# Joining the two halves of an attention value product: two scalar-engine copies and two vector additions from PSUM, or four copies and one addition in SBUF

## The chip, the cores and the metric

The kernel runs on one core of a Trainium2 chip. The core has five engines that run side by side, each with its own in-order queue: the tensor engine TensorE (PE in the profile, with PEld for its weight loads), the vector engine VectorE (DVE), the scalar engine ScalarE (ACT), GpSimdE (POOL) and the sync engine SyncE (SP), which only issues DMAs here. TensorE writes its products to PSUM, a small memory of banks of 128 x 512 float32; DVE and ACT read PSUM, POOL does not. Everything else works on SBUF. The metric is the device time of one execution in microseconds (us), less is better; the time of a kernel is the median of its runs.

## The reference

One decoder layer over 1024 tokens with 1024 channels. Its two token mixers run in parallel from one input projection: sliding-window attention (16 query heads, 4 key/value heads of width 64, window 128, one sink logit per head) and a gated delta rule (8 heads of width 128). Both are projected, gated, summed and projected again, and a squared-ReLU MLP follows. What matters here is the attention:

```python
def _sliding_window_attention(q, k, v, sinks):
    ...
    kb, vb = band(k), band(v)                 # each block of 128 tokens sees itself and the block before
    scores = jnp.einsum('bnqhgd,bnshd->bnhgqs', qb, kb).astype(jnp.float32) * (ATT_HEAD_DIM ** -0.5)
    ...
    m = jnp.maximum(jnp.max(scores, axis=-1, keepdims=True), sink)
    p = jnp.exp(scores - m)
    denom = jnp.sum(p, axis=-1, keepdims=True) + jnp.exp(sink - m)
    probs = (p / denom).astype(v.dtype)
    o = jnp.einsum('bnhgqs,bnshd->bnqhgd', probs, vb)
    return o.reshape(b, s, ATT_Q_W)
```

The last product, `probs` times `vb`, is the one whose result is joined.

## The kernel before

The kernel reaches float32 accuracy with a faster matmul format by splitting: a tensor is kept as a high part and a low part (the remainder), and a product is three matmuls (high by high, high by low, low by high). ACT copies the high part, DVE subtracts to get the low one.

**The stage.** The attention is not a stage of its own. It is woven into a long run of projections (`stream_unit`, 26 units of 48 matmuls of 128 x 512 on the three PSUM banks called `mm`; line 248). `count[0]` is the number of such matmuls issued so far, and it is the clock of the program: `at(p, f)` puts a function into a heap under the count `p`, `after(n, f)` puts it `n` counts on, and `run_events` calls what is due before each projection matmul. So the order on TensorE, DVE and ACT is written out by hand through these numbers (`manual_schedule`); POOL's order is left to the framework's scheduler.

**A slot.** There are 64 slots, one for each pair of heads `j = s // 8` and block of 128 queries `n = s % 8`, 16 counts apart. A slot has three parts on TensorE, each with its followers on the other engines:

- `att_scores(s)` at the slot's count: four matmuls into a bank of tag `a` (two banks; lines 834 and 835), then `top` (DVE, masks and takes the maximum, `nscore`, line 842), `expo` (ACT, exponentials, line 849), `join` (POOL, adds the two halves of the window, `sm`, line 853), `inv` (DVE, reciprocal of the sum, line 856) and `scale` (ACT, line 861).
- `att_turn(s)` at +28: two transposes of `sm` into a bank of tag `b` (two banks; line 877), then the high copy (ACT, `ph`, line 883), the low part (DVE, line 887) and a masked copy `pl` (POOL, line 894).
- `att_values(s)` at +62: the product with the values into the only bank of tag `c` (line 909): two matmuls with `ph` and, for `n > 0`, two with `pl`. It is this product that is joined.

**The value product and its join.** The left operand of line 909 is a tile of 128 columns: 64 columns are the high part of the values and 64 are the low part. So rows 0 to 63 of the bank hold one partial sum and rows 64 to 127 the other, for two heads side by side (columns 0 to 127 and 128 to 255), and the answer is their sum. The kernel does this with an ACT copy and two DVE additions:

```python
def top():
    A.activation(out=bot, in_=av[64:128, 0:256], func=AF.Copy)          # line 914
    after(4, join)
def join():
    ...
    for i in range(2):
        V.tensor_tensor(out=o[64 * i:64 * i + 64, (n % 2) * P:(n % 2 + 1) * P],   # line 922
                        in0=av[0:64, i * P:(i + 1) * P], in1=bot[:, i * P:(i + 1) * P], op=ALU.add)
```

`o` is a 128 x 256 tile `at` that takes the two heads of two slots; on every odd slot POOL issues a DMA of it to DRAM (`attn_d`, line 925). `bot` and `at` have two buffers each.

**What else is in DVE's queue in this stage.** Low parts of weights (`wl`, line 216) and of queries (`qs`, line 803), and the steps of a triangular solve (`stt`, line 732, and `M`, line 737), 128 rows by up to about a thousand elements, which are strewn over the same counts.

After slot 63, `open_pc` releases these pools, DVE clears a tile there (`TT`, line 965), and the delta-rule heads begin.

Of the kernel before, what the change touches and what calls it, by code (L numbers as in the profile page):

```python
# [9 lines left out]
F32 = mybir.dt.float32  # L10
F32R = mybir.dt.float32r
BF16 = mybir.dt.bfloat16
AF = mybir.ActivationFunctionType
ALU = mybir.AluOpType
# [3 lines left out]
P = 128  # L18
# [16 lines left out]
def hybrid_layer_kernel(ctx: ExitStack, tc: tile.TileContext,  # L35
                        x, c, w_ada, b_ada, w_in, conv_w, a_log, dt_bias, sinks, dn_norm_w,
                        w_oa, w_ob, w_out, ln1_g, ln1_b, w_ff1, b_ff1, w_ff2, b_ff2,
                        ln2_g, ln2_b, out, dbg=None):
    nc = tc.nc
    x, c, out = x[0], c[0], out[0]  # L40
# [6 lines left out]
    V, A, G, T = nc.vector, nc.scalar, nc.gpsimd, nc.tensor  # L47
# [7 lines left out]
    def psum(tag, bufs, name=None):  # L55
        return ps.tile([P, HALF], F32, tag=tag, bufs=bufs, name=name or tag)
# [4 lines left out]
    def bc(ap, shape):  # L61
        return ap.to_broadcast(shape)
# [134 lines left out]
    def at(p, f, *args):  # L197
        order[0] += 1
        heapq.heappush(events, (p, order[0], f, args))

    def after(n, f, *args):
        at(count[0] + n, f, *args)
# [275 lines left out]
    for step in ('t0 s0 o00 o01 w0 w1 d4 t1 s1 v203 o10 v235 o11 v256 m0 t2 p2 s2 v304 o20 v346 o21 m1 t3 p3 s3 v404 o30 v446 o31 m2 '  # L478
                 't4 p4 s4 v504 o40 v546 o41 m3 t5 p5 s5 r0 v604 o50 v646 o51 m4 t6 p6 s6 v704 o60 v746 o61 m5 t7 p7 s7 o70 o71 m6').split():
        f, k = step[0], int(step[1])  # L480
# [44 lines left out]
    with tc.tile_pool(name="pa", bufs=2, side="right") as pa:  # L525
        if True:
# [76 lines left out]
            for half in range(2):  # L603
                gr = psum("a", 2)
                for j in range(4):
# [3 lines left out]
                                in1=gT[0:8, halves[half]].bitcast(F32), op=ALU.subtract)  # L609
# [42 lines left out]
        for h in range(8):  # L652
# [7 lines left out]
            for half in range(2):  # L660
                tp = psum("c", 1) if half else psum("b", 2)
                for j in range(4):
                    n = 4 * half + j
                    T.transpose(tp[:, j * P:(j + 1) * P], kT[:, n * P:(n + 1) * P], ident)
                for j in range(4):
                    n = 4 * half + j
# [11 lines left out]
            for half in range(2):  # L678
                V.tensor_tensor(out=kd[:, halves[half]].rearrange("p (n c) -> p n c", n=4),
                                in0=tps[half].rearrange("p (n c) -> p n c", n=4),  # L680
                                in1=bc(kdc[:, 4 * half:4 * half + 4, h:h + 1], [P, 4, P]), op=ALU.mult)
            (nc.sync if h == 7 else nc.gpsimd).dma_start(out=kd_d[h], in_=kd)
            for half in range(2):
                kk = psum("a", 2)
                for j in range(4):
                    n = 4 * half + j
                    kc = kT[:, n * P:(n + 1) * P]
                    T.matmul(kk[:, j * P:(j + 1) * P], lhsT=kc, rhs=kc, start=True, stop=True)
                for j in range(4):
                    n = 4 * half + j  # L690
# [20 lines left out]
    pb = pb_pool.__enter__()  # L711
# [104 lines left out]
    att = {}  # L816
# [84 lines left out]
    def att_values(s):  # L901
        j, n = s // 8, s % 8
        full, part = att.pop(s)
        av = psum("c", 1)
        vt = vhl[j // 2]
        prods = [(VB[n], full)] + ([(n, part)] if n else [])
        for b, p_ in prods:
            for m in range(2):
                T.matmul(av[:, 0:256], lhsT=vt[:, b, :], rhs=p_[:, m, :], start=p_ is full and m == 0,  # L909
                         stop=p_ is prods[-1][1] and m == 1)  # L910
        bot = pb.tile([64, 256], F32, tag="bot", name="bot")

        def top():
            A.activation(out=bot, in_=av[64:128, 0:256], func=AF.Copy)
            after(4, join)

        def join():
            if n % 2 == 0:
                att["at"] = pb.tile([P, 2 * P], F32, tag="at", name="at")
            o = att["at"]  # L920
            for i in range(2):
                V.tensor_tensor(out=o[64 * i:64 * i + 64, (n % 2) * P:(n % 2 + 1) * P],
                                in0=av[0:64, i * P:(i + 1) * P], in1=bot[:, i * P:(i + 1) * P], op=ALU.add)
            if n % 2 == 1:
                nc.gpsimd.dma_start(out=attn_d[j, :, (n - 1) * P:(n + 1) * P], in_=o)

        after(5, top)

    def slot(s):
        return int(SLOT0 + SLOT * s)  # L930
# [1 line left out]
    for s in range(64):  # L932
        at(slot(s), att_scores, s)
        at(slot(s) + TURN, att_turn, s)
        at(slot(s) + VAL, att_values, s)
# [568 lines left out]
    for s in range(4):  # L1504
# [4 lines left out]
        for ts in groups:  # L1509
            pts = []  # L1510
            for t in ts:
                tag = ("mm", "a", "mm", "c", "mm", "a")[bank % 6]
# [135 lines left out]
    def acc_tag(i, ab):  # L1648
        if i < EARLY:
            return {"A": "mm" if i < 3 else "b", "B": "aacaa"[i], "C": "caaca"[i]}[ab]  # L1650
        return {"A": "mm", "B": "a", "C": "b"}[ab]
# [203 lines left out]
    for i, m in seq:  # L1855
# [4 lines left out]
        if begin:  # L1860
            tag = acc_tag(i, ab)
# [146 lines left out]
```

## Time and profile before

| | |
|---|---|
| median of 3 runs | 1879.66 us (1875.06 to 1884.38) |
| the profiled execution | 1881.81 us, its span 1880.1 us |
| granted TensorE clock over the span | 0.99 |
| busy time of PE, DVE, ACT, POOL | 1826.4, 1306.0, 977.6, 339.2 us |
| first and last start of a `ph` matmul of the value product (line 909) | 257.4 and 568.9 us |
| matmuls of the value product (`ph`, `pl`) | 128 and 112 |
| ACT copies of line 914 | 64, 64 x 256, 382 ns each |
| DVE additions of line 922 | 128, 64 x 128, 278 ns each |
| DMA issues of `attn_d` (line 925) | 32 |

The span is from the first to the last instruction; what the execution's own time has beyond it lies around them. A group's row in the profile reads: line, engine, operation, output <- inputs, shapes, count | busy us, mean ns of one | idle time of that engine before them and what ended it. A row of the timeline reads: start us, us until the end, engine, line, operation, tiles, shapes, count, and in brackets the idle time before it with its releaser. Matmul ends are modelled: a 128 x 512 matmul shows 0.39 us, and yet the next one starts some 0.23 us after it. A row of the waits reads: who waited <- for whom: us in total, times, longest.

### The profile page before, as it was taken

Reading aid. Unit: us, or ns where it says so; the run is one execution under the profiler, and the core shown is the slowest. Engines: PE = TensorE matmul, PEld = TensorE weight load, DVE = VectorE, ACT = ScalarE, POOL = GpSimd, SP = SyncE. Lnnn points to the kernel's source line nnn. Section 1 sums busy time; section 2 is a strip of 40 time slices with the busy share of each in tenths; the row PEclk is TensorE's granted clock in tenths of the full one; section 3 lists DMA queues with packets and bytes.
Section 4 is the critical chain, followed back from the end, with each engine's and each line's share of the span. In section 5 each row is a group of like instructions: output and inputs, shape, how many; then the busy total and the mean of one; then the engine's idle time right before and its main releaser. Section 6 shows DMA issues by size and latency. Waiting matters only on the chain.

```text
span 1880.1 us, 26086 instructions
## 1 busy us (share of the span) xinstructions
PE 1826.4 (97%) x9161; PEld 1507.9 (80%) x9161; DVE 1306.0 (69%) x2473; ACT 977.6 (52%) x2105; POOL 339.2 (18%) x493
## 2 busy tenths in 40 slices
PE   7999999999999999999999999999999999999997
PEld 5877878878787878888878888877878787888886
DVE  7777588898875566666553445787867776576697
ACT  3689656666664454454553332465545555334441
POOL 7323323443331000000001110001221220000000
PEclk8999999999999999999999999999999999999999
DMA  9655642232248444544345644358978779755571
GB/s 260 171 183 199 214 100 77 84 98 70 68 170 227 127 139 134 159 149 144 118 157 187 205 141 151 123 168 279 311 240 282 261 244 396 281 196 170 198 259 45
DMA packets 262414, 337.74 MB, mean 180 GB/s; under 512 B 26005, under 2 KB 171110, under 8 KB 262026
## 3 DMA queue, kind: packets, MB, share of 16 engines
q1 hardware_dynamic: 222954, 212.94, 36.1%
q0 software_dynamic: 31328, 108.44, 17.1%
q10 hardware_dynamic: 8000, 14.68, 2.1%
q8 instruction: 72, 1.18, 0.3%
q14 instruction: 60, 0.49, 0.1%
HBM read 231.40 MB, written 102.51 MB: 178 GB/s over the span
## 4 chain that ended last, share of the span: by engine, by line
PE 77%; DVE 10%; DMA 5%; ACT 4%; issue 3%; SPq 1%; POOL 0%; ACTq 0%; DVEq 0%; POOLq 0%
PE mm L248 31%; PE mm L1929 6%; PE mm L1869 5%; PE b L1929 4%; PE a L1929 4%; PE b L1869 3%; PE c L1929 2%; PE a L1869 2%; PE mm L1499 2%; PE c L909 1%; DMA sraw<-in_w_ff_dram 1%; DVE wl L216 1%; PE mm L188 1%; PE mm L187 1%; PE mm L186 1%
## 5 line engine op out<-in xcount | busy, mean ns | idle before, releaser
L248 PE MATMUL mm<-uh,wl 128*128 128x512 f32 x800 | 332.3, 415 | 0.0
L248 PE MATMUL mm<-ul,wh 128*128 128x512 f32 x800 | 321.9, 402 | 0.0
L248 PE MATMUL mm<-uh,wh 128*128 128x512 f32 x800 | 318.4, 398 | 0.0
L216 DVE TENSOR_TENSOR sp<-sraw,sp 128x1024 fp32r<-128x1024 f32 x112 | 132.7, 1220 | 78.6 <-ACT sp L215 78.6
L215 ACT ACTIVATE sp<-sraw 128x1024 fp32r<-128x1024 f32 x112 | 112.8, 1054 | 124.0 <-PE b L1929 75.4
L248 PEld LDWEIGHTS mm<-ul,wh 128*128 128x128 f32 x800 | 151.4, 189 | 26.8 <-issue 0.2
L248 PEld LDWEIGHTS mm<-uh,wl 128*128 128x128 f32 x800 | 152.0, 190 | 23.1 <-issue 3.9
L248 PEld LDWEIGHTS mm<-uh,wh 128*128 128x128 f32 x800 | 151.7, 190 | 21.5 <-issue 0.2
L1929 PE MATMUL mm<-sp 128*128 128x512 f32 x528 | 137.3, 390 | 1.7 <-DVE sp L216 1.0
L1929 PEld LDWEIGHTS mm<-sp 128*128 128x128 f32 x528 | 98.4, 188 | 23.3 <-DVE sp L216 2.2
L216 DVE TENSOR_TENSOR wl<-wr,wh 128x1024 fp32r<-128x1024 f32 x81 | 98.6, 1218 | 7.5 <-ACT wh L215 7.5
L215 ACT ACTIVATE wh<-wr 128x1024 fp32r<-128x1024 f32 x81 | 85.1, 1050 | 22.0 <-PE c L1499 13.9
L1929 PE MATMUL a<-sp 128*128 128x512 f32 x336 | 92.6, 389 | 0.0
L1929 PE MATMUL b<-sp 128*128 128x512 f32 (+1 forms) x336 | 80.0, 374 | 0.0
L1169 ACT ACTIVATE vn<-a,brk 128x128 f32<-128x128 f32 x64 | 23.6, 368 | 108.1 <-PE a L1167 107.1
L842 DVE CUSTOM_DVE_ANT_0 nscore<-a,amask,nsink 128x256 f32<-128x256 f32 (+1 forms) x128 | 54.6, 464 | 34.6 <-PE a L835 33.8
L216 DVE TENSOR_TENSOR wl<-fraw,wh 128x1024 fp32r<-128x1024 f32 x43 | 52.5, 1222 | 35.5 <-ACT wh L215 35.2
L1929 PEld LDWEIGHTS a<-sp 128*128 128x128 f32 x336 | 63.1, 188 | 13.2
L853 POOL TENSOR_TENSOR sm<-sm 128x256 f32<-128x256 f32 x56 | 55.7, 994 | 99.0 <-ACT sm L849 66.2
L1929 PEld LDWEIGHTS b<-sp 128*128 128x128 f32 x336 | 60.5, 188 | 11.2
L849 ACT ACTIVATE sm<-nscore,stat 128x257 f32<-128x257 f32 (+1 forms) x128 | 62.1, 488 | 4.2 <-DVE stat L842 3.7
L894 POOL TENSOR_SCALAR_AFFINE_SELECT pl<-ph 128x512 fp32r<-128x512 f32 x56 | 44.0, 785 | 90.4 <-DVE ph L887 71.6
(524 smaller groups left out, 4678.0 us busy)
## 6 DMA issues: line engine op xcount, KB each, us to landing
wr<-in_w_in_dram SPq DMA_DIRECT2D x60, 512.0 KB, 3.6
sraw<-hf_d SPq DMA_DIRECT2D x54, 512.0 KB, 4.0
fraw<-in_w_ff_dram SPq DMA_DIRECT2D x32, 512.0 KB, 4.9
sraw<-wt_d SPq DMA_DIRECT2D x32, 512.0 KB, 4.4
hf_d<-t ACTq DMA_DIRECT2D x48, 256.0 KB, 4.2
wt_d<-wx POOLq DMA_DIRECT2D x48, 256.0 KB, 3.8
sraw<-in_w_ff_dram SPq DMA_DIRECT2D x22, 512.0 KB, 5.3
adaw<-in_w_ada_dram SPq DMA_DIRECT2D x41, 256.0 KB, 2.8
```

Of the source, the lines that this page charges most:

```text
L186: T.matmul(t, lhsT=wh[:, k, :], rhs=xh[k][:, sl], start=k == 0, stop=False)
L215: A.activation(out=hi, in_=src, func=AF.Copy)
L216: after(lag, lambda: V.tensor_tensor(out=lo, in0=src, in1=hi.bitcast(F32), op=ALU.subtract))
L248: T.matmul(ts[half], lhsT=w[:, k, :], rhs=xx[k][:, sl], start=k == 0 and m == 0, stop=k == KT - 1 and m == 2)
L842: V.tensor_tensor_reduce(out=ns[:, i, 1:1 + W], in0=sc[:, i * 2 * P:i * 2 * P + W], in1=amask[:, mo:mo + W], scale=-1.0, scalar=nsink[:, 2 ...
L849: A.activation(out=sm[:, i, 0:1 + W], in_=ns[:, i, 0:1 + W], func=AF.Exp, scale=-1.0, bias=st[:, i:i + 1], accum_out=st[:, 2 + i:3 + i])
L853: G.tensor_tensor(out=sm[:, :, 1 + P:1 + 2 * P], in0=sm[:, :, 1:1 + P], in1=sm[:, :, 1 + P:1 + 2 * P], op=ALU.add)
L894: G.affine_select(out=flat4(part), in_=flat4(full), pattern=[[0, 4], [1 if odd else -1, P]], compare_op=ALU.is_ge if odd else ALU.is_gt, f ...
L1169: after(1, lambda: A.activation(out=vn, in_=Wp[:, 0:P], func=AF.Copy, scale=brk[:, n, h:h + 1]))
L1499: T.matmul(pt, lhsT=m[k][:, tok], rhs=w[:, k % 2, :], start=k == 0 and w is wh and m is mh, stop=k == KT - 1 and m is ml)
L1869: T.matmul(pt, lhsT=a[:, k0 + k, :], rhs=b[k], start=begin and k == 0 and x_ == 0, stop=k == 3 and x_ == 2, skip_group_check=True)
L1929: T.matmul(to, lhsT=a[:, f, t * P:(t + 1) * P], rhs=b[:, f, lo:up], start=(begin or own) and s % NS == 0 and f == 0 and x_ == 0, stop=s % ...
```

## The change

ACT now copies all four quarters of the bank to SBUF, each 64 x 128: the low rows of both heads into `bot`, the high rows into `at`, so that each head's two partial sums lie on the same 64 partitions. DVE then adds `bot` to `at` in place, once, over 128 x 128, and reads only SBUF. `bot` is a 128 x 128 tile in place of 64 x 256, and `at` is taken when the value product is issued instead of when the join is. The join falls due 5 counts after the copies in place of 4.

```diff
-        bot = pb.tile([64, 256], F32, tag="bot", name="bot")
-
-        def top():
-            A.activation(out=bot, in_=av[64:128, 0:256], func=AF.Copy)
-            after(4, join)
+        if n % 2 == 0:
+            att["at"] = pb.tile([P, 2 * P], F32, tag="at", name="at")
+        o = att["at"]
+        bot = pb.tile([P, P], F32, tag="bot", name="bot")
+        sl = slice((n % 2) * P, (n % 2 + 1) * P)
+
+        def copy():
+            for i in range(2):
+                for k, dst in ((1, bot), (0, o[:, sl])):
+                    A.activation(out=dst[64 * i:64 * i + 64, :], in_=av[64 * k:64 * k + 64, i * P:(i + 1) * P], func=AF.Copy)
+            after(5, join)
 
         def join():
-            if n % 2 == 0:
-                att["at"] = pb.tile([P, 2 * P], F32, tag="at", name="at")
-            o = att["at"]
-            for i in range(2):
-                V.tensor_tensor(out=o[64 * i:64 * i + 64, (n % 2) * P:(n % 2 + 1) * P],
-                                in0=av[0:64, i * P:(i + 1) * P], in1=bot[:, i * P:(i + 1) * P], op=ALU.add)
+            V.tensor_tensor(out=o[:, sl], in0=o[:, sl], in1=bot, op=ALU.add)
             if n % 2 == 1:
                 nc.gpsimd.dma_start(out=attn_d[j, :, (n - 1) * P:(n + 1) * P], in_=o)
 
-        after(5, top)
+        after(5, copy)
```

Three places show what moves. The first is TensorE's queue at the value product of slot 1, with the semaphores that each row waits for (`DVE`, `PE` and `Activation` are the engines that raise them). Before:

```order
L248 MATMUL mm<-ul_136,wh 128x512
L877 MATMUL b<-ident,sm 128x128 [waits Activation_49] x2
L248 MATMUL mm<-uh_128,wl 128x512
L248 MATMUL mm<-uh_129,wh 128x512
L909 MATMUL c<-ph,vhl 128x256 [waits DVE_49,PE_49]
L909 MATMUL c<-ph,vhl 128x256
L909 MATMUL c<-pl,vhl 128x256 x2
```

And with the change:

```order
L248 MATMUL mm<-ul_136,wh 128x512
L877 MATMUL b<-ident,sm 128x128 [waits Activation_49] x2
L248 MATMUL mm<-uh_128,wl 128x512
L248 MATMUL mm<-uh_129,wh 128x512
L909 MATMUL c<-ph,vhl 128x256 [waits PE_49]
L909 MATMUL c<-ph,vhl 128x256
L909 MATMUL c<-pl,vhl 128x256 x2
```

The order is the same; the value product no longer waits for DVE. It does not name ACT either, because the transposes two counts ahead of it (line 877) already wait for an ACT instruction that stands behind the copies in ACT's queue, as the second place shows. It is ACT's queue around one slot; before:

```order
L914 ACTIVATE bot<-c 64x256 [waits PE_49]
L861 ACTIVATE sm<-sm,stat 128x128 [waits DVE_49,Pool_49]
L861 ACTIVATE sm<-sm,stat 128x128 [waits Activation_49]
L811 ACTIVATE gate<-mm 128x512 [waits PE_49]
L849 ACTIVATE sm,stat<-nscore_2090,stat 128x257 [waits DVE_49] x2
L883 ACTIVATE ph<-b 128x256 [waits PE_49,Pool_49]
```

And with the change:

```order
L920 ACTIVATE bot<-c 64x128 [waits PE_49]
L920 ACTIVATE at<-c 64x128
L920 ACTIVATE bot<-c 64x128
L920 ACTIVATE at<-c 64x128
L861 ACTIVATE sm<-sm,stat 128x128 [waits DVE_49,Pool_49]
L861 ACTIVATE sm<-sm,stat 128x128 [waits Activation_49]
```

The four copies stand where the one stood, right ahead of the scaling of `sm` (line 861) whose result the next transposes read. The third place is DVE's queue at the first join, as a difference:

```order
 L842 ISA stat 128x1
 L887 TENSOR_TENSOR ph<-b,ph 128x256
-L922 TENSOR_TENSOR at<-c,bot 64x128 x2
+L924 TENSOR_TENSOR at<-at,bot 128x128
 L732 TENSOR_TENSOR stt<-M 128x612
 L737 TENSOR_TENSOR M<-M,stt 128x12x51
```

One addition stands in place of two, between the low part of `ph` and the steps of the solve; in a few slots it falls one solve step later.

## The prediction

> **What bounds the kernel now.** I read the page first, then the waits of TensorE in the attention stage, then the timeline of one slot that waits and one that does not.
>
> ```profile
> PE 1826.4 (97%) x9161; PEld 1507.9 (80%) x9161; DVE 1306.0 (69%) x2473; ACT 977.6 (52%) x2105; POOL 339.2 (18%) x493
> ...
> PE 77%; DVE 10%; DMA 5%; ACT 4%; issue 3%; SPq 1%; POOL 0%; ACTq 0%; DVEq 0%; POOLq 0%
> ```
>
> TensorE is the bound of the whole kernel, by its busy share and by the chain that ended last. So an edit to the join is worth only what TensorE waits because of it. TensorE's waits in the stretch from 255 to 580 us (these two rows are all), and then the group of the value product (shortest, median and longest in ns, first and last start):
>
> ```profile
> PE c L909 <- DVE at L922: 6.2, 9, 1.5
> PE c L909 <- issue: 0.4, 1, 0.4
> ```
>
> ```profile
> L909 PE MATMUL c<-ph,vhl x128: 277/282/358, 257.4 to 568.9; 128*128 128x256 f32 x128
> ```
>
> In this stage TensorE waits for one thing: the additions of the join, before it may write the single bank `c` again. DVE is late there because its queue runs full, as the windows (us, then busy us and instructions of PE, PEld, DVE, ACT, POOL, the clock, DMA) show with 52 of 60 us:
>
> ```profile
> 260.00:320.00 60.00, 59.15 (x314) 49.24 (x313) 52.54 (x132) 40.48 (x119) 22.36 (x28) 1.00 0.23 75
> ...
> 380.00:440.00 60.00, 58.39 (x310) 48.67 (x310) 53.73 (x130) 41.51 (x122) 25.43 (x34) 1.00 0.32 96
> ```
>
> The longest of these waits in the timeline, TensorE first, then DVE:
>
> ```profile
> 331.27 0.40 PE L909 MATMUL c<-ph,vhl 128*128 128x256 f32 x2
> ...
> 336.11 0.40 PE L909 MATMUL c<-ph,vhl 128*128 128x256 f32 x2
> ...
> 340.51 0.40 PE L248 MATMUL mm<-ul,wh 128*128 128x512 f32 x1
> 342.38 0.48 PE L909 MATMUL c<-ph,vhl 128*128 128x256 f32 x2 [1.47 <-DVE at L922]
> ```
>
> ```profile
> 338.30 1.22 DVE L216 TENSOR_TENSOR wl<-wr,wh 128x1024 fp32r<-128x1024 f32 x1
> 339.55 0.68 DVE L803 SCALAR_TENSOR_TENSOR qs<-mm,qs 64x512 fp32r<-64x512 f32 x1
> 340.26 1.15 DVE L737 TENSOR_TENSOR M<-M,stt 128x950 f32<-128x950 f32 x1
> 341.33 0.42 DVE L887 TENSOR_TENSOR ph<-b,ph 128x256 fp32r<-128x256 f32 x1
> 341.66 0.57 DVE L922 TENSOR_TENSOR at<-c,bot 64x128 f32<-64x128 f32 x2
> ```
>
> Three long instructions of DVE stand ahead of the join, which ends at 342.23 us, and the value product starts 0.15 us later. An unhindered slot takes 336.11 - 331.27 = 4.84 us.
>
> **The change part by part.** *The stall.* A wait's row undercounts, because a matmul's shown end is late: the matmul at 340.51 would have been followed at 340.74 (0.23 us on), so 1.64 us are lost where the row says 1.47; and the first pair behind a stall shows 0.48 in place of 0.40. That is some 0.25 us a stall beside the rows. Stepping through the timeline I find 13 late starts of line 909 (three too short to have a row): 6.6 + 13 x 0.25 = 9.8 us. A second count: the last product's pair shows 568.9 for its second matmul, so it starts at 568.8, and 63 steps from 257.4 are 311.4 us. At 4.84 they would be 304.9; eight of them follow a slot without the two `pl` matmuls (4 x 0.12 us a slot for four matmuls, so 0.24 less each: 1.9), the last three hold no score matmuls (0.48 each: 1.4), and two of these no transposes (0.24 each: 0.5). That leaves 301.1, and 10.3 us lost. I take 9.8. The change removes the cause: the bank is free when ACT's fourth copy ends, whatever DVE does.
>
> *Is ACT a worse releaser?* The prices, from the groups by form and two rows of ACT's timeline:
>
> ```profile
> L914 ACT ACTIVATE bot<-c 64x256 f32<-64x256 f32 x64 | 24.4, 382 | 5.4 <-issue 2.7 <-PE c L909 1.3
> ...
> L1193 ACT ACTIVATE junk<-c 128x128 f32<-128x128 f32 x64 | 17.6, 275 | 34.2 <-PE c L1190 34.1
> ```
>
> ```profile
> 338.24 0.38 ACT L914 ACTIVATE bot<-c 64x256 f32<-64x256 f32 x1
> 338.52 0.68 ACT L861 ACTIVATE sm<-sm,stat 128x128 f32<-128x128 f32 x2
> ```
>
> A 64 x 128 copy is not in the trace; the 128 x 128 read of the same bank, 275 ns, is its nearest row, since the partitions run side by side. The follower of a 382 ns copy starts 0.28 us after it, so 0.10 overlaps, and a 128-element copy holds ACT for 0.175 us. Four take 0.70 against 0.28: 0.42 us more a slot (0.82 if nothing overlapped, the upper end; the lower, if the extra three cost only their elements, 0.2). The bank is freed about 0.42 us later after ACT's start than a single copy ends. The shortest distance of that kind in the whole stage is this one:
>
> ```profile
> 562.33 0.38 ACT L914 ACTIVATE bot<-c 64x256 f32<-64x256 f32 x1
> ...
> 564.70 0.40 PE L909 MATMUL c<-ph,vhl 128*128 128x256 f32 x2
> ```
>
> From the copy's end at 562.71 there are 1.99 us to the next product. So ACT never holds the bank up, at either price: cost 0.
>
> *What is queued behind the copies.* The scaling of `sm`, and through it the transposes, TensorE's next chance to wait. Three slots are tight (ACT's scalings, then the transposes that they release):
>
> ```profile
> 299.74 0.70 ACT L861 ACTIVATE sm<-sm,stat 128x128 f32<-128x128 f32 x2 [1.82 <-DVE stat L856]
> ...
> 380.04 0.70 ACT L861 ACTIVATE sm<-sm,stat 128x128 f32<-128x128 f32 x2 [1.28 <-DVE stat L856]
> ...
> 464.87 0.70 ACT L861 ACTIVATE sm<-sm,stat 128x128 f32<-128x128 f32 x2 [1.93 <-DVE stat L856]
> ```
>
> ```profile
> 300.62 0.38 PE L877 MATMUL b<-ident,sm 128*128 128x128 f32 x2
> ...
> 380.98 0.38 PE L877 MATMUL b<-ident,sm 128*128 128x128 f32 x2
> ...
> 465.88 0.38 PE L877 MATMUL b<-ident,sm 128*128 128x128 f32 x2
> ```
>
> The slack is 0.18, 0.24 and 0.31 us; everywhere else I find 0.7 or more. In all three ACT had been idle and waited for DVE's reciprocal, so the longer copies cost nothing there. But each lies just behind a removed stall of about 0.57 us. If DVE is no earlier than now, TensorE runs ahead by that much and loses 0.57 - slack: 0.39 + 0.33 + 0.26 = 1.0 us. If DVE is 0.28 us a join earlier, nothing. I take 1.0.
>
> *DVE's own time.* Two additions of 0.57 us together go, one comes:
>
> ```profile
> L922 DVE TENSOR_TENSOR at<-c,bot 64x128 f32<-64x128 f32 x128 | 35.6, 278 | 6.4 <-ACT bot L914 5.5
> ```
>
> ```profile
> L737 DVE TENSOR_TENSOR M<-M,stt 128x122 f32<-128x122 f32 x1 | 0.3, 285 | 0.0
> ```
>
> 122 elements from SBUF take 285 ns, so 128 take about 0.29: 0.28 less a slot, 18 us over 64, if nothing interferes. But the new addition has both inputs in SBUF, and rows show what that does between DVE and POOL:
>
> ```profile
> 345.62 0.64 POOL L894 TENSOR_SCALAR_AFFINE_SELECT pl<-ph 128x512 fp32r<-128x512 f32 x1 [3.03 <-DVE ph L887]
> ...
> 348.38 0.73 POOL L853 TENSOR_TENSOR sm<-sm 128x256 f32<-128x256 f32 x1 [1.56 <-ACT sm L849]
> ...
> 350.92 1.62 POOL L853 TENSOR_TENSOR sm<-sm 128x256 f32<-128x256 f32 x1
> ```
>
> ```profile
> 342.99 1.17 DVE L732 TENSOR_TENSOR stt<-M 128x962 f32<-128x962 f32 x1
> ...
> 346.00 1.26 DVE L737 TENSOR_TENSOR M<-M,stt 128x962 f32<-128x962 f32 x1
> ```
>
> The same POOL addition takes 0.73 us alone and 1.62 beside solve steps; the 962-element solve step takes 1.17 us alone and 1.26 when it starts in the middle of POOL's `pl`. Today the join, which reads PSUM, runs beside `pl` unhindered and the solve step behind it starts when `pl` is half done. With a shorter join the step starts 0.28 us earlier, but `pl` still holds it. So I count DVE's gain as about 0 of a possible 18 us; the bounds are a gain of 0.28 a slot and a loss of up to the 0.73 that POOL may be in front. Of itself this is off TensorE's path: cost 0.
>
> The Trainium skill says this outright in "SBUF — State Buffer", section "Who interferes with whom": a DVE instruction with two SBUF inputs contends with a GpSimd instruction that reads SBUF, and the one that issues second blocks for all of the first. It speaks against the change, and the 1.62 beside 0.73 agrees with it for POOL as the loser; by that rule alone the join could cost more than the pair it replaces.
>
> *The end of the stage.* The last join releases the pools, and later TensorE waits once for DVE there:
>
> ```profile
> PE b L1145 <- DVE E L1131: 2.0, 1, 2.0
> ```
>
> The copies come 0.42 us later and the join ends 0.28 sooner; the whole chain hangs on slot 63 and moves with it: 0.
>
> *Sum.* 9.8 - 1.0 = 8.8 us less: 1881.8 becomes 1873.0 for the profiled execution (span 1880.1 and 1.7 around it). That execution is 2.2 us above the median of the runs; from 1879.66 it is 1870.9.
>
> **The rivals.** *The wait moves to the transposes.* With the bank free, TensorE's next partner is the chain exponentials, POOL's `sm`, reciprocal, scaling. ACT adds 0.42 us to it, POOL up to 0.9 (1.62 - 0.73) when the join is in front. For it: the three tight slots. Against: slack of 0.7 to 3 us elsewhere, and ACT idle in most slots. If the chain were later by 1.3 us everywhere, most of the 13 leads would be lost again; I put that at 6 of 9.8: 1875.9, and anything up to no gain.
>
> *Slower: DVE becomes the bound.* If a join meets POOL's `sm` (wait up to 0.73) and pushes the next solve step behind `pl` (0.64), DVE spends up to 0.29 + 0.73 + 0.64 = 1.66 where it spent 0.57, 1.09 more. DVE is idle for 60 - 52.54 = 7.5 us in 60, 0.6 us a slot; the rival decides beyond that. At the full price 64 x 0.49 = 31 us more stage, less the 10 us that it holds as stalls today: +21, 1901; at 0.8 a slot +3, 1883. For it: the port rows. Against: the join follows line 887, which itself releases `pl`, so POOL mostly starts behind the join and not ahead of it.
>
> *It does nothing.* If the value product waited for something else that ends just as late, the stalls would stay: 1880. Against: the order shows no DVE wait left on it, and `ph` and `pl` are finished several us ahead.
>
> **How the numbers follow.** Forecast 0.62, moved wait 0.26, DVE-bound 0.08, nothing 0.04. What a measurement here can tell from no change is about 0.5%, 9.4 us, so the line lies at 1870.3, close to the forecast: I give 0.38 of the forecast's chance to faster and 0.24 to the same, and 0.02 of the moved wait to faster. Faster 0.40, same 0.53, slower 0.07. The forecast's own range is 1866 to 1876 (gain of 10.3 and the runs' scatter below, 4 above); taking in most of the moved wait and a little of the slower case gives 1864 to 1882.
>
> **What would show it.** In the profile after: no row of line 909 waiting for DVE or ACT between 255 and 570 us; the value product's first and last start 301 to 304 us apart in place of 311.4; copies of 270 to 285 ns; a join of about 290 ns by its shortest; waits of line 877 for ACT of 2 us or less in total. If line 877 waits 5 us or more, the moved wait is right; if joins average over 0.6 us and DVE's idle time before `nscore` is gone, the slower rival is. A gain with the distance of 311 us unchanged would prove the reading of the stage wrong.

## The result, and the profile after

The changed kernel took 1869.83 us (median of 7 runs, 1865.69 to 1877.13), the kernel before 1881.31 us on the same chip (7 runs, 1875.06 to 1884.38). The ratio is 0.9946 with a 95% interval of [0.9927, 0.9964]: about 0.5% faster. The interval lies wholly below 1, and a gain of 0.5% lies inside it. A second comparison, told with the experiments, gave 0.9958 [0.9944, 0.9972].

The profiled execution of the change took 1877.13 us, with a span of 1875.1. It is the slowest of its seven, so its span says less of the change than the stage does. The page's busy times and its chain that ended last:

```profile
PE 1826.1 (97%) x9161; PEld 1509.8 (81%) x9161; DVE 1291.1 (69%) x2409; ACT 1022.9 (55%) x2297; POOL 351.5 (19%) x493
...
PE 79%; DVE 8%; ACT 5%; DMA 5%; issue 2%; SPq 1%; POOL 0%; ACTq 0%; DVEq 0%; POOLq 0%
```

TensorE still bounds the kernel. DVE has 14.9 us less work (1306.0 before), ACT 45.3 more (977.6), POOL 12.3 more (339.2). What TensorE gained is read in the attention stage. First the windows after (us, then busy us and instructions of PE, PEld, DVE, ACT, POOL, the clock, DMA share and GB/s); the same two stretches as were shown of before:

```profile
260.00:320.00 60.00, 60.00 (x323) 50.48 (x321) 50.79 (x116) 48.61 (x153) 27.17 (x29) 1.00 0.23 75
...
380.00:440.00 60.00, 59.95 (x321) 50.41 (x320) 51.35 (x116) 50.12 (x158) 30.20 (x33) 1.00 0.32 97
```

TensorE is now busy all the time (59.15 and 58.39 before). ACT pays with 8 us more in 60. The group of the value product after (shortest, median and longest in ns, first and last start), and what is left of TensorE's waits for this stage, with the wait of ACT's scaling for DVE's reciprocal:

```profile
L909 PE MATMUL c<-ph,vhl x128: 274/280/283, 255.9 to 558.5; 128*128 128x256 f32 x128
```

```profile
ACT sm L861 <- DVE stat L856: 8.9, 9, 1.6
...
PEld b L877 <- ACT sm L861: 2.4, 12, 0.5
```

The longest value product fell from 358 to 283 ns, and no row of line 909 waits for anything. First and last start lie 558.5 - 255.9 = 302.6 us apart, against 568.9 - 257.4 = 311.5 in the same row before: 8.9 us gained. What stands there instead are twelve short waits of the weight load of line 877 for the scaling. Summed over the starts of the transposes against their usual distance, TensorE loses 1.1 us by them.

Of the other engines, the groups by form after (busy us, mean ns of one, then idle time before them and its releasers):

```profile
L894 POOL TENSOR_SCALAR_AFFINE_SELECT pl<-ph 128x512 fp32r<-128x512 f32 x56 | 64.8, 1157 | 75.1 <-DVE ph L887 57.8 <-PE b L877 6.5 <-PE mm L248 3.6
...
L920 ACT ACTIVATE bot<-c 64x128 f32<-64x128 f32 x128 | 35.0, 274 | 5.3 <-PE c L909 3.2
L920 ACT ACTIVATE at<-c 64x128 f32<-64x128 f32 x128 | 34.7, 271 | 1.5
...
L924 DVE TENSOR_TENSOR at<-at,bot 128x128 f32<-128x128 f32 x64 | 22.6, 353 | 7.2 <-ACT at L920 7.1
```

and the one row before that answers to the first of them:

```profile
L894 POOL TENSOR_SCALAR_AFFINE_SELECT pl<-ph 128x512 fp32r<-128x512 f32 x56 | 44.0, 785 | 90.4 <-DVE ph L887 71.6 <-PE b L877 10.8 <-PE mm L248 7.9
```

The four copies take 2 x (274 + 271) ns = 1.09 us a slot, the join 0.353 where the pair took 0.56. POOL's `pl` went from 785 to 1157 ns. Followed one by one in the two traces, 32 of the 56 `pl` now start while a solve step of DVE (lines 732 and 737) is running, 9 before; each of these lasts 0.49 to 0.51 us longer than what is left of that step, where a free one takes 0.64 us in all. So it is the solve step, which now starts earlier, that `pl` waits for. The new join is hardly a part of it: with that addition taken off DVE (the run with the join on POOL, below) `pl` still takes 1087 ns. POOL has the time (27 of 60 us busy).

One more view of after is needed below, the timeline of ACT with one set of copies and the scaling behind it:

```profile
335.55 0.27 ACT L920 ACTIVATE bot<-c 64x128 f32<-64x128 f32 x1
335.83 0.27 ACT L920 ACTIVATE at<-c 64x128 f32<-64x128 f32 x1
336.12 0.27 ACT L920 ACTIVATE bot<-c 64x128 f32<-64x128 f32 x1
336.40 0.27 ACT L920 ACTIVATE at<-c 64x128 f32<-64x128 f32 x1
336.70 0.70 ACT L861 ACTIVATE sm<-sm,stat 128x128 f32<-128x128 f32 x2
```

The copies follow each other at 0.28 to 0.29 us although each shows 0.27, and the scaling starts 0.03 us after the last one: nothing overlaps. From the first copy to the scaling are 1.15 us.

Where the 8.9 us are afterwards: followed by single matmuls that both traces hold, after is 10.4 us ahead of before at the end of attention (1.5 of it stood there already when the stage began), 12.6 at 610 us and 12.7 at 1240, but only 5.5 at 1561, in the last long matmul stage. Most of that stage's loss belongs to the one execution, as a second profile shows; the windows of after and of before, first after:

```profile
1360.00:1420.00 60.00, 56.32 (x233) 45.67 (x232) 40.00 (x56) 29.63 (x43) 13.54 (x25) 0.94 0.70 231
1420.00:1480.00 60.00, 58.01 (x249) 47.49 (x249) 41.32 (x57) 30.45 (x45) 12.97 (x24) 0.97 0.82 274
```

```profile
1360.00:1420.00 60.00, 56.32 (x239) 45.59 (x239) 39.25 (x54) 30.08 (x44) 11.82 (x22) 0.97 0.78 263
1420.00:1480.00 60.00, 60.00 (x266) 49.55 (x264) 43.78 (x60) 32.34 (x47) 11.49 (x22) 1.00 0.75 253
```

TensorE was granted 0.94 and 0.97 of its clock there, against 0.97 and 1.00, and waited 2 us more. A second profiled execution of the change (below) lost 2.1 us there in place of 7.2. The medians differ by 11.5 and 7.4 us, around the 8.9 of the stage; the runs do not show what the rest on either side is made of.

### The profile page after: what moved, and what is told of

It is laid out like the page before. It is cut to its first block, busy times and chain, and to the rows that moved or that the text cites. A ratio compares the mean times of both kernels' runs of the same rounds, so it can differ in the third digit from the quotient of the medians.

```text
span 1875.1 us, 26152 instructions
## 1 busy us (share of the span) xinstructions
PE 1826.1 (97%) x9161; PEld 1509.8 (81%) x9161; DVE 1291.1 (69%) x2409; ACT 1022.9 (55%) x2297; POOL 351.5 (19%) x493
## 4 chain that ended last, share of the span: by engine, by line
PE 79%; DVE 8%; ACT 5%; DMA 5%; issue 2%; SPq 1%; POOL 0%; ACTq 0%; DVEq 0%; POOLq 0%
PE mm L248 33%; PE mm L1930 6%; PE mm L1870 5%; PE b L1930 4%; PE a L1930 4%; PE b L1870 3%; PE a L1870 2%; PE c L1930 2%; PE mm L1500 2%; PE c L909 1%; DMA hf_d<-t 1%; PE mm L188 1%; PE mm L187 1%; PE mm L186 1%; DMA sraw<-in_w_ff_dram 1%
## 5 line engine op out<-in xcount | busy, mean ns | idle before, releaser
L894 POOL TENSOR_SCALAR_AFFINE_SELECT pl<-ph 128x512 fp32r<-128x512 f32 x56 | 64.8, 1157 | 75.1 <-DVE ph L887 57.8
L853 POOL TENSOR_TENSOR sm<-sm 128x256 f32<-128x256 f32 x56 | 49.5, 884 | 96.0 <-ACT sm L849 53.3
```

The source lines that it names most:

```text
L853: G.tensor_tensor(out=sm[:, :, 1 + P:1 + 2 * P], in0=sm[:, :, 1:1 + P], in1=sm[:, :, 1 + P:1 + 2 * P], op=ALU.add)
L894: G.affine_select(out=flat4(part), in_=flat4(full), pattern=[[0, 4], [1 if odd else -1, P]], compare_op=ALU.is_ge if odd else ALU.is_gt, f ...
```

## The experiments

The theory after the result: TensorE gains because ACT, not DVE, is the last to read the bank; ACT's longer copies and POOL's longer `pl` lie beside other work. The rivals: that DVE's shorter work is what counts, and the release is not; that the copies are a cost that only happens to be hidden. All variants below start from the changed kernel, and each was run on one chip beside the kernel before, whose medians were 1880.47 us for the first four, 1881.57 for the next four and 1882.91 for the last two.

### DVE again the last reader of the bank

```diff
             for i in range(2):
                 for k, dst in ((1, bot), (0, o[:, sl])):
-                    A.activation(out=dst[64 * i:64 * i + 64, :], in_=av[64 * k:64 * k + 64, i * P:(i + 1) * P], func=AF.Copy)
+                    w = 120 if i and not k else P
+                    A.activation(out=dst[64 * i:64 * i + 64, 0:w], in_=av[64 * k:64 * k + 64, i * P:i * P + w], func=AF.Copy)
...
         def join():
+            V.tensor_copy(out=o[64:128, sl][:, 120:P], in_=av[0:64, P + 120:2 * P])
             V.tensor_tensor(out=o[:, sl], in0=o[:, sl], in1=bot, op=ALU.add)
```

> The changed kernel, but DVE copies the last 8 of the 512 columns of the four quarters from PSUM itself, just ahead of its addition; ACT copies the rest. DVE's work on a join stays below that of before (about 0.2 + 0.29 us against 0.57), but the bank is again free only when DVE has been there. Theory (the gain is the release of the bank by ACT): the stalls of line 909 for DVE come back, 5 to 8 us of waits, the value products' first and last start about 310 us apart (311.4 before, 302.6 with the change), time 1877 to 1884 us, ratio 0.997 to 1.003. Rival (the gain is DVE's shorter work): most of the gain stays, distance 302 to 305 us, ratio about 0.995.

Measured: 1883.22 us (12 runs), ratio 1.000 [0.9985, 1.0016]. The distance of the value products is 567.4 - 255.6 = 311.8 us, that of before. TensorE's wait, and the slot that answers to the one shown of before:

```profile
PE c L909 <- DVE at L925: 5.1, 8, 1.1
```

```profile
340.85 0.42 DVE L887 TENSOR_TENSOR ph<-b,ph 128x256 fp32r<-128x256 f32 x1
341.30 0.16 DVE L925 COPY at<-c 64x8 f32<-64x8 f32 x1
...
341.61 0.47 PE L909 MATMUL c<-ph,vhl 128*128 128x256 f32 x2 [1.15 <-DVE at L925]
```

DVE reads eight columns of the bank in 0.16 us, at the place in its queue where the join stands, and the whole gain is gone. Summed over the starts of the value product against their usual distance, TensorE loses 9.0 us at the bank here, 9.6 before and nothing in the change; at the transposes it loses 0.7. So which engine releases the bank decides. One thing is not as meant: DVE's work did not get smaller. The join took 531 ns on average here (353 in the change), with the copy's 159 more than the 0.56 of the pair. So part of the copy's lateness may be DVE's heavier load (215.4 of the 240 us from 260 to 500, 208.5 before); the next run, in which DVE has still more to do, has no such wait. The wait's own row names the copy, which is over before the join begins.

### Two additions in place of one

```diff
-            V.tensor_tensor(out=o[:, sl], in0=o[:, sl], in1=bot, op=ALU.add)
+            for i in range(2):
+                r = slice(64 * i, 64 * i + 64)
+                V.tensor_tensor(out=o[r, sl], in0=o[r, sl], in1=bot[r, :], op=ALU.add)
```

> The changed kernel with the addition done as two of 64 x 128 from SBUF, so that DVE's work on a join is that of before (about 0.57 us and the port besides) and ACT still frees the bank. Theory (release by ACT): no wait of line 909, distance of the value products 302 to 304 us, ratio 0.993 to 0.997, as the change itself. Rival (DVE's shorter work): the gain goes, distance about 310 us, ratio 0.998 to 1.002. Third (DVE becomes the bound once two SBUF additions meet POOL): waits for DVE's reciprocal at line 861 grow above 20 us and the distance exceeds 311 us.

Measured: 1877.23 us (12 runs), ratio 0.9981 [0.9965, 0.9997]; distance 567.8 - 259.2 = 308.6 us. Its waits and the group of its additions:

```profile
ACT sm L861 <- DVE stat L856: 27.4, 24, 2.2
PEld b L877 <- ACT sm L861: 9.5, 28, 1.4
PE b L877 <- ACT sm L861: 2.4, 4, 1.0
```

```profile
L926 DVE TENSOR_TENSOR at<-at,bot 64x128 f32<-64x128 f32 x128 | 59.8, 467 | 8.1 <-ACT at L920 6.2
```

This missed what the theory expected. No row of line 909 waits, so the release works, yet 6 of the 8.9 us are gone. They went where the first rival of the prediction had seen them: ACT's scaling waits 27.4 us for DVE's reciprocal (8.9 in the change), and the transposes wait for the scaling. The two additions cost 0.93 us a slot, more than the pair before (0.56), 467 ns for each where 278 stood, beside a `pl` of POOL that is short again (730 ns). So the release pays in full only while DVE has room: DVE at 224.8 of the 240 us from 260 to 500 (208.5 before, 203.6 in the change) is late for the reciprocal in its place. By its ratio and its distance this run lies where the rival had put it, that DVE's shorter work is what counts, or nearly; by its waits it does not, because not one of them is at the bank. Of the third possibility, DVE as the bound, the sign at the reciprocal came (27.4 us, over 20), but not the distance of over 311 us. Nor can shorter work of DVE be what is left of the gain, since DVE works 281.6 us between the first and the last value product here, 262.2 before and 248.3 in the change. What shorter work would be worth with DVE still the last at the bank, no run shows.

### Two copies of both quarters, one addition of 64 x 256

```diff
-            att["at"] = pb.tile([P, 2 * P], F32, tag="at", name="at")
+            att["at"] = pb.tile([64, 2, 2 * P], F32, tag="at", name="at")
...
-        bot = pb.tile([P, P], F32, tag="bot", name="bot")
+        bot = pb.tile([64, 2, P], F32, tag="bot", name="bot", bufs=1)
...
-            for i in range(2):
-                for k, dst in ((1, bot), (0, o[:, sl])):
-                    A.activation(out=dst[64 * i:64 * i + 64, :], in_=av[64 * k:64 * k + 64, i * P:(i + 1) * P], func=AF.Copy)
+            for k, dst in ((1, bot), (0, o[:, :, sl])):
+                A.activation(out=dst, in_=av[64 * k:64 * k + 64, 0:2 * P].rearrange("p (i c) -> p i c", i=2), func=AF.Copy)
...
-            V.tensor_tensor(out=o[:, sl], in0=o[:, sl], in1=bot, op=ALU.add)
+            V.tensor_tensor(out=o[:, :, sl], in0=o[:, :, sl], in1=bot, op=ALU.add)
...
-                nc.gpsimd.dma_start(out=attn_d[j, :, (n - 1) * P:(n + 1) * P], in_=o)
+                nc.gpsimd.dma_start(out=attn_d[j, :, (n - 1) * P:(n + 1) * P].rearrange("(i p) c -> p i c", i=2), in_=o)
```

> The changed kernel with two ACT copies of 64 x 256 (0.39 us each) in place of four of 64 x 128 (0.28 each), one DVE addition of 64 x 256, a single buffer for bot, and the output DMA from 64 partitions. ACT saves 0.35 us a slot. Theory (what is left at the transposes, 2.4 us in 12 waits on ACT, is ACT's copies standing ahead of the scaling): these waits fall below 1 us, distance 301 to 302 us, ratio 0.992 to 0.996, 0 to 2 us less than the change. Rival (the rest at the transposes is set by DVE's reciprocal): they stay at 2 us or more and the distance stays 302.6 or grows, since the single buffer makes ACT wait for DVE.

Measured: 1876.30 us (12 runs), ratio 0.997 [0.9956, 0.9984]; distance 558.9 - 256.7 = 302.2 us. Two waits of TensorE, one in the stage and one behind it:

```profile
PEld b L877 <- ACT sm L861: 1.2, 5, 0.5
```

```profile
PE b L1088 <- DMA T<-t_d: 4.1, 1, 4.1
```

The group of the addition:

```profile
L923 DVE TENSOR_TENSOR at<-at,bot 64x256 f32<-64x256 f32 x64 | 30.6, 479 | 6.6 <-ACT at L919 6.5
```

The addition takes 0.48 us a slot, more than the 0.35 of the change and less than the 0.56 of the pair before, and the stage gains 9.3 us all the same.

The copies take 381 and 378 ns, 0.33 us a slot less than the four. In the stage that is worth 0.4 us by the distance. The waits stayed above the 1 us that was expected, and the ratio above the 0.996. In this execution TensorE stood 4.1 us at the start of the delta-rule heads for a transfer; whether that is why the time is not better is not shown. The wait is followed up below.

### Every copy twice

```diff
-                for k, dst in ((1, bot), (0, o[:, sl])):
+                for k, dst in ((1, bot), (0, o[:, sl])) * 2:
```

> The changed kernel with each of ACT's four copies done twice: 1.14 us more ACT work a slot. Theory (the copies are free only because ACT idles; in the changed kernel it is busy 50 of 60 us, 4.0 of 4.84 a slot): ACT needs about 5.2 us a slot and becomes the bound, distance of the value products 315 to 330 us, TensorE waiting for ACT at the transposes, ratio 1.002 to 1.012. Rival (ACT has ample room, what counts is only that DVE is out of the release): distance below 305 us and ratio 0.994 to 0.997.

Measured: 1900.08 us (4 runs), ratio 1.0093 [1.0069, 1.0118]; distance 584.3 - 255.4 = 328.9 us. As the theory expected, ACT becomes the bound. TensorE's waits in the stage:

```profile
PEld b L877 <- ACT sm L861: 32.1, 57, 1.8
PE b L877 <- ACT sm L861: 15.5, 28, 1.4
PEld c L909 <- ACT at L920: 0.3, 1, 0.3
```

1.14 us more of ACT a slot cost 26.3 us, 0.41 us a slot, and nearly all at the transposes, hardly at the bank. TensorE is over 0.3 us late there in 29 of the 64 slots, and ACT had been idle before the scaling in only 2 of the 64. So the copies cost little only because ACT has room for this much; of the next 1.14 us, 0.41 have to be paid.

### The change once more, and three variants

> The change itself, once more beside the three that follow, so that they are compared on one chip. Theory (the stall at the bank is gone and about 1 us is lost at the transposes; the rest of the profiled execution's shortfall came from its late stages): 0.9925 to 0.9965 of the time before, the value products' first and last start 302 to 304 us apart, and the mark at the end of the attention stage some 10 us earlier than before. Rival (the 8.9 us are given back in the later stages, as the one profiled execution shows): the same distance, but under 6 us less in the whole.

Measured, all as the theory expected: 1874.14 us (6 runs), ratio 0.9958 [0.9944, 0.9972]; distance 558.9 - 256.3 = 302.6 us and 1.1 us lost at the transposes, both as in the first profile. After followed 10.0 us ahead at the end of attention, 10.8 at 610 and 10.0 at 1240 us, and 7.9 at 1561: the gain of the stage arrives in the later ones, and what the last long stage takes from it differs between two executions of one kernel by 5 us.

The addition on POOL in place of DVE:

```diff
-            V.tensor_tensor(out=o[:, sl], in0=o[:, sl], in1=bot, op=ALU.add)
+            G.tensor_tensor(out=o[:, sl], in0=o[:, sl], in1=bot, op=ALU.add)
```

> The addition of the join goes from DVE to POOL; everything else is as in the change. The theory that DVE's time counts as well as the release (from the run with two additions, which lost 6 us at the transposes because DVE's reciprocal came late) expects DVE to have some 0.35 us more a slot, so late reciprocals do not occur, and the distance of the value products at 301.5 to 303.5 us, ratio 0.992 to 0.997. A rival: POOL is in order, and an addition that waits for ACT's copies, or runs for about 0.5 us ahead of the sum of sm, delays the chain to the transposes by as much; then line 877 waits for ACT over 5 us in all and the distance is 305 to 310.

Measured: 1872.40 us (6 runs), ratio 0.9947 [0.9932, 0.9961]; distance 557.4 - 255.2 = 302.2 us. Its wait at the transposes and its join:

```profile
PEld b L877 <- ACT sm L861: 1.6, 8, 0.5
```

```profile
L924 POOL TENSOR_TENSOR at<-at,bot 128x128 f32<-128x128 f32 x64 | 40.3, 630 | 77.2 <-ACT at L920 77.1
```

With the join off DVE altogether (190.7 us busy of the 240, 203.6 in the change) the stage is 0.4 us shorter, and no late reciprocal decides a transpose any more. POOL waits 77 us for the copies without being missed. So to take more work off DVE than the change does is worth next to nothing, while the two additions, which give it more, cost 6 us. Somewhere between the 0.48 us a slot of the single addition of 64 x 256, which loses nothing, and the 0.93 of the two the price begins; where was not measured.

The copies behind the scaling:

```diff
-        after(5, copy)
+        after(9, copy)
```

> The four copies are issued four steps later, behind the scaling of sm in ACT's queue. Theory (the 1.1 us that the change still loses at the transposes come from the copies' 1.14 us ahead of the scaling, and the bank has about 2 us of room): no wait of line 909, line 877's waits for ACT at or below those of the change, and the distance of the value products 301.5 to 303. Rival (the bank has less room than the one slot I measured): line 909 waits again, for ACT, and the distance is 305 or more.

Measured: 1879.93 us (12 runs), ratio 0.9999 [0.9985, 1.0013]; distance 564.6 - 256.8 = 307.8 us. The waits, and one slot:

```profile
PEld c L909 <- ACT at L920: 7.2, 13, 0.8
PE c L909 <- ACT at L920: 1.9, 7, 0.4
```

```profile
303.75 0.70 ACT L861 ACTIVATE sm<-sm,stat 128x128 f32<-128x128 f32 x2 [0.51 <-POOL sm L853]
304.47 0.28 ACT L920 ACTIVATE bot<-c 64x128 f32<-64x128 f32 x1
...
305.32 0.27 ACT L920 ACTIVATE at<-c 64x128 f32<-64x128 f32 x1
...
305.64 0.30 PEld L909 LDWEIGHTS c<-ph,vhl 128*128 128x128 f32 x2 [0.41 <-ACT at L920]
```

The rival was right: the product waits at the bank again, now for ACT. No transpose is held by ACT's queue any more, as meant, but behind a scaling that itself waits for POOL or DVE the copies come too late. DVE's work is that of the change (248.8 us between the first and the last value product), and yet the stage gains only 3.7 us: shorter work of DVE does not do it alone. In the change at least 1.25 us lie between the last copy's end and the next value product; that room belongs to the copies' place in front of the scaling, not to ACT as such.

Two copies, with the last pair's output by SP's queue:

```diff
-                nc.gpsimd.dma_start(out=attn_d[j, :, (n - 1) * P:(n + 1) * P].rearrange("(i p) c -> p i c", i=2), in_=o)
+                (nc.sync if s == 63 else nc.gpsimd).dma_start(out=attn_d[j, :, (n - 1) * P:(n + 1) * P].rearrange("(i p) c -> p i c", i=2), in_=o)
```

> As the run with two copies of 64x256 and one addition of 64x256, but the last pair's output goes out by SP's queue in place of POOL's. Theory: the 4.1 us that TensorE waited there for the triangular blocks (T) at the start of the delta-rule heads hang on the landing of that last output, which holds the memory of the next stage; if it lands earlier by about 1 us or more, the wait shrinks to 0 to 3 us and the time is 0.992 to 0.996 of the time before, at or below the change. Rival: that wait was bad luck in the order of the transfers and has nothing to do with the output; then it stays at 3 to 5 us, or is gone without the landing being earlier.

Measured: 1873.80 us (7 runs), ratio 0.9957 [0.9942, 0.9972]; distance 558.1 - 255.9 = 302.2 us. The wait for T is gone, and the next stage's first load starts at 563.99 in place of 566.05 us, 0.8 of it because this execution's value products end that much earlier. That fits the theory, but does not show it: the second profile of the change started the same load at 566.17 us and had no such wait either.

### Two copies again, and the two mildest edits together

> The run with two copies of 64x256 and POOL's queue for every output, once more. In its first profile TensorE waited 4.1 us for T at the start of the delta-rule heads: T's two transfers took 10.5 us on average to land, against 6.9 to 7.1 in the change and with the output by SP. If that belongs to the kernel (the order or the time of its transfers), line 1088 waits 3 to 5 us for T again and T lands in over 10 us. If it is a chance state of the transfers, T lands in some 7 us, no such wait is there, and the time is that of the run with the output by SP: 0.993 to 0.997 of the time before.

Measured: 1874.88 us (12 runs), ratio 0.9964 [0.9946, 0.9982]; distance 561.5 - 259.2 = 302.3 us. The issue of T's two transfers (KB each, mean us to landing), in the first profile of this kernel and then in this one:

```profile
T<-t_d SPq DMA_DIRECT2D x2, 64.0 KB, 10.5
```

```profile
T<-t_d SPq DMA_DIRECT2D x2, 64.0 KB, 8.6
```

The same program, and no wait of line 1088 for T this time, though T landed later than the 7 us expected: the 4.1 us do not belong to the program, but to the transfers of one execution. The profile of the copies behind the scaling had a wait like it (3.4 us, T landing in 10.2). What makes T land in 7 us once and in 10.5 another time stays open; neither the moment of its issue nor the way of the last output explains it.

The join on POOL and the last pair's output by SP's queue:

```diff
-            V.tensor_tensor(out=o[:, sl], in0=o[:, sl], in1=bot, op=ALU.add)
+            G.tensor_tensor(out=o[:, sl], in0=o[:, sl], in1=bot, op=ALU.add)
...
-                nc.gpsimd.dma_start(out=attn_d[j, :, (n - 1) * P:(n + 1) * P], in_=o)
+                (nc.sync if s == 63 else nc.gpsimd).dma_start(out=attn_d[j, :, (n - 1) * P:(n + 1) * P], in_=o)
```

> The join's addition on POOL, and the last pair's output by SP's queue: the two edits that left the least waiting so far. Theory: the value products' distance is as with the join on POOL (302.1 to 302.5 us), the next stage's memory is free up to 1 us earlier, and the time is 0.992 to 0.996 of the time before: with what can be told here no better than the change itself (0.9944 to 0.9972). If it were 0.992 or less, the end of the stage would be worth more than I read from it.

Measured: 1870.71 us (7 runs), ratio 0.9944 [0.9924, 0.9965]; distance 553.6 - 251.5 = 302.1 us. As expected no version can be told from the change itself: its two ratios and those of the variants that keep the 302 us all lie between 0.9944 and 0.9970, with intervals that overlap.

## Why the prediction was right

**The stall.** Right. The prediction took 9.8 us off for it. All its rows are gone. The run in which DVE reads only eight columns of the bank brings them back, 9.0 us at the bank, and the run with two additions, where DVE is busier still but ACT is the last reader, has none of them. Together they show that the release, and not DVE's shorter work, ends the wait at the bank. To keep the whole gain DVE must have room besides, since the two additions give 6 us back at the transposes.

**The loss at the transposes.** Right in its sum, 1.1 us for the 1.0 predicted, partly by luck, since it is mostly wrong in its places. (The row of waits reads 2.4 us, a little over the 2 that the prediction allowed; a wait's row is not the loss.) Of the three slots named only the first loses (0.3 us at 298.5 us). The other losses are at 308.6 (0.16) and 395.5 us (0.45) and in crumbs of at most 0.05. The prediction said that the longer copies cost nothing at the transposes, because ACT waits for the reciprocal in the tight slots; ACT's queue is what ends last in 8 of the 11 tight slots after, and the shorter copies of the run with two give 0.4 us back.

**The copies.** This term was mis-sized. The prediction took 0.175 us for a copy, from a 382 ns copy whose follower starts 0.28 us later, and so 0.42 us a slot. Measured is 0.28 a copy, 1.15 us from the first copy to the scaling, 0.87 more than before: a little over the upper end of 0.82, given for no overlap at all. The follower in the row that was used is the scaling, an instruction of another kind; a copy behind a copy does not start early. (The Trainium skill says in "ScalarE: Activation LUTs", section "What ACT_TABLE_LOAD costs", that back-to-back ACTIVATEs overlap by some 93 ns. These traces show that for the scaling behind a copy of 64 x 256, 0.10 us. They do not show it for a copy behind a copy, nor for the scaling behind a copy of 64 x 128, which starts 0.03 us after the copy's end; for these the measurement decides. What the overlap hangs on stays open.) It cost little, since most of the 0.87 still fits ACT's room. The doubled copies show the limit: 1.14 us more cost 26 us. The other claim of that step, that ACT never holds the bank up, held at the larger price too. The copies behind the scaling show on what it rests: on their place in the queue.

**DVE's time.** The step counted about 0 of a possible 18 us, because POOL's `pl` would hold the solve step back. The groups show 35.6 - 22.6 = 13.0 us less for the join, and DVE's sum is 14.9 us smaller. The step that failed is the order of the two: the solve step mostly starts ahead of `pl` now, so it is `pl` that is held, at 1157 ns in place of 785. The join is at 281 ns by its median and 849 at its worst; 20 of the 64 start while POOL works and average 0.51 us. The Trainium skill says in "SBUF — State Buffer", section "Who interferes with whom", that of two such instructions the one that issues second is blocked; the traces agree (a join of 0.83 us at 309.9, 0.2 us after POOL's `sm` began, and a `pl` of 1.63 at 342.9, just after a solve step began), and give the sizes. "Of itself this is off TensorE's path: cost 0" was half right. Less DVE time than the change's gives almost nothing more (0.4 us with the join on POOL). But more of it is not free: at 0.93 us a slot for two additions 6 of the 8.9 us go at the transposes. So the first rival, the wait that moves to the transposes, was nearer than its place in the prediction told: some 0.4 us of DVE a slot beyond what stood there before are enough to bring most of it.

**The end of the stage.** Counted as 0. From the last value product to 610 us (by the marks of before) the change gained 2.2 us in one profile and 0.8 in the other. The two profiles of the version with two copies lost 4.0 and 0.8 there. With such a scatter within one program, nothing of it can be put down to the change.

**The sum and the range.** 8.8 us were predicted, the stage gives 8.9, and the two comparisons 11.5 and 7.4 us between medians. 1869.83 lies 1.1 us below the predicted 1870.9. That closeness is partly luck: the prediction started from a median before of 1879.66 us, which seven runs put at 1881.31, and the medians then differ by 2.7 us more than was predicted. That the result would fall on the line between "faster by 0.5%" and "the same" was the forecast, and it did. The rival in which DVE becomes the bound needed joins of over 0.6 us; they average 0.353.

## What to carry to other kernels

When an engine of the critical path waits for a single-buffered PSUM bank, look at which engine's queue reads it last: eight columns read by a late queue cost as much as the whole addition, and a copy by an engine with room takes the wait away. Then ask what stands behind that copy in the releaser's queue and how much room that queue has, since the same copies cost next to nothing in front of the scaling, brought the wait back behind it, and cost 26 us when doubled. Price a follower only by a row in which the same two kinds of instruction, of the same sizes, follow each other.

## What the runs showed of the hardware that I had not expected

- ACT's small copies from PSUM run strictly one after the other: 271 to 274 ns each, 0.28 to 0.29 us from start to start. Four of 64 x 128 take 1.09 us and two of 64 x 256 take 0.76, so half the elements take 0.71 of the time of one. The scaling behind a copy of 64 x 256 starts 0.10 us before that copy's shown end, and behind a copy of 64 x 128 it starts 0.03 us after it.
- An addition of 64 partitions from SBUF took 467 ns on average beside POOL's work, one of 128 partitions with as many elements a row 353, and one of 64 x 256 479. In the first case POOL's `pl` stayed short (730 ns), in the other two it paid (1157 and 1357). Between `pl` and a solve step the order of their starts matters: a `pl` that starts while a solve step runs lasts until 0.5 us after that step's end, in 32 cases of the change and 9 of before. In the run with two additions, 71 of the 128 start while POOL works and average 0.62 us; the others take 0.28.
- The same two transfers of 64 KB, issued at about the same point, landed in 6.9 to 10.5 us on average in different executions; where they landed in over 10, TensorE waited 3.4 and 4.1 us for them at the start of the next stage. A single profile of the whole is no measure of a gain of that size; the distance between two marks within the stage repeated to 0.1 us.
